# A hybrid attention layer on one core: per-unit maxima and delayed exponentials in the differential heads

## The chip, the core and the metric

The kernel runs as one program on one NeuronCore of one Trainium2 chip. The core has a matrix engine (TensorE, PE in the profile; its weight loads stand apart as PEld), a vector engine (VectorE, DVE), an activation engine (ScalarE, ACT), a Pool engine (GpSimd, POOL) and a queue for transfers (SyncE, SP). Each engine takes its own instructions strictly one after the other and waits on semaphores for the results of the others. The metric is the device time of one execution in microseconds, the median of several executions.

## The reference

One decoder layer for 2048 tokens of width 1024, all in float32. Two groups of attention heads read the same normalised input; only the first group matters here.

```
n  = rms_norm(x, norm_g)
dq, dk, dv, ... = split(n @ w_in)              # 4 differential heads, 2 maps each of width 64, values 128
q, k = rope(dq), rope(dk);  scale = 64 ** -0.5 # = 0.125
sc = einsum(q, k) * scale                      # two score maps m = 0, 1 per head
pr = softmax(where(k_idx <= q_idx, sc, -inf))  # causal
a  = pr[0] - lam * pr[1]                       # one learned lam
od = rms_norm(a @ v, subln_g) * 0.8, then * silu(gate)
... second group (latent attention, 8 heads), output projection, gated embedding, final norm
```

## The kernel before

The program runs in stages, one after the other: the input projection (0 to about 470 us), the up projections of the latent group (to about 650), latent attention (to about 1162), the differential heads (1162 to 1576), and the output stage (to 2040). Tiles come from pools with a fixed number of buffers; a compile-time scheduler puts each engine's instructions in order from the order in the source and from when it thinks their inputs are there, and sets all semaphores.

**Projection of queries and keys (L359 to L385).** For m = 0 (queries) and m = 1 (keys) the product of 512 tokens by 128 columns lands in PSUM tile `ps`; VectorE multiplies it by a cosine table (L375, one instruction) and by a sine table (L377, four instructions of 32 partitions), Pool adds both (L379), and the sum is split in two parts and stored.

**Differential heads (L810 to L1005).** Work comes in blocks `(h, b)`: head h, 128 query rows b, keys up to n = 128 (b + 1). `block` (L845) makes the unnormalised weights of one block. Its scores are computed in units of up to 1024 keys, so a block with b of 8 or more has two units per map (`nu` = 2), the others one. `unit(m, u)` (L854) multiplies queries with keys into the PSUM tile `pu` (1024 columns, three buffers, L816), and VectorE takes the row maximum (L874). Before, the units of one map come one after the other, and `expo(m)` (L876) follows when both are there: one small VectorE instruction turns the larger maximum into the bias (L880 for two units, L882 for one), and ScalarE takes the exponentials of both units with the scale 0.125 and sums them (L885). So the first unit's PSUM buffer is held until the second unit's maximum is known. `combine` (L888) runs after the first unit of the next block: sums (L891), reciprocals (L893), the factor `cc` (L895), and then map 0 plus `cc` times map 1: the last unit by VectorE (L902), a full first unit by Pool in two instructions (L899 multiplies map 1, L900 adds).

`weigh(h, g)` (L913) takes blocks 2g and 2g + 1: per 256 keys, `turn` transposes the weights on PE into the PSUM tile `tpa` (one buffer, L930), ScalarE copies it to `ah` (L932), and `mul` multiplies with the values (L942). At the end come a copy, a transpose, squares on ScalarE (L956), a power on Pool (L107) and two small pairs of VectorE instructions (L961, L962); the Pool power and those pairs are put in as `ends` at places 2 and 4 of the following task list (L991).

The main loop (L982) runs over 32 pairs (h, g); even heads go up in g, odd heads go down. In step i, `merge` weaves the tasks of `weigh` with those of two blocks that lie three ahead (`LEAD`), by their costs. During the last head the loads and splits of the output weights (L835 to L837) are woven in too. In the first head pair and again in the second, 16 blocks have two units, 32 in all; the other 32 blocks have one.

Of the kernel before, what the change touches and what calls it, by code (L numbers as in the profile page):

```python
# [8 lines left out]
F32 = mybir.dt.float32  # L9
# [4 lines left out]
ALU = mybir.AluOpType  # L14
# [11 lines left out]
LAM_INIT = 0.2  # L26
TWO_PI = 6.283185307179586
# [37 lines left out]
def tile_hymba(ctx, tc, a, out):  # L65
# [130 lines left out]
    with ExitStack() as c1:  # L196
# [162 lines left out]
        for m in range(2):  # L359
            wg, wn = wn, (load_w(512, 512) if m == 0 else load_w(2560, 272))  # L360
            for t in range(NT):
# [4 lines left out]
                for g in range(4):  # L366
# [8 lines left out]
                    V.tensor_mul(t1, pt, tcos)  # L375
                    for q in range(4):
                        V.tensor_mul(t2[32 * (q ^ 1):32 * (q ^ 1) + 32], pt[32 * q:32 * q + 32],  # L377
                                     tsin[32 * q:32 * q + 32])
# [431 lines left out]
    SC_D = 64.0 ** -0.5  # L810
    with ExitStack() as c3:
# [32 lines left out]

        def block(h, b):  # L845
# [8 lines left out]
            def unit(m, u):  # L854
                hd = heads[h]
                if m == 0 and u == 0:
                    st["s"] = sm.tile([P, 2, 2], F32, name="ssum", tag="ssum", bufs=4)
                if u == 0:
                    st[m] = pp.tile([P, S], F32, name="pb", tag=f"pb{m}", bufs=(6 if m == 0 else 2))
                    st["x", m] = sm.tile([P, 2], F32, name="mxd", tag="mxd", bufs=4)  # L860
                pu = ps_s.tile([P, 1024], F32, name="pu")
                st["u", m, u] = pu
# [11 lines left out]
                V.reduce_max(st["x", m][:, u:u + 1], pu[:, :w], axis=AX.X)  # L874

            def expo(m):  # L876
                mx, ssum = st["x", m], st["s"]
                nm = sm.tile([P, 1], F32, name="nm", tag="nm", bufs=4)
                if nu == 2:
                    V.tensor_scalar(nm, mx[:, 0:1], scalar1=mx[:, 1:2], scalar2=-SC_D, op0=ALU.max, op1=ALU.mult)  # L880
                else:
                    V.tensor_scalar_mul(nm, mx[:, 0:1], -SC_D)  # L882
                for u in range(nu):
                    w = min(1024, n - u * 1024)
                    A.activation(st[m][:, u * 1024:u * 1024 + w], st["u", m, u][:, :w], AF.Exp, scale=SC_D, bias=nm,  # L885
                                 accum_out=ssum[:, m, u:u + 1])

            def combine():  # L888
                ssum = st["s"]
                if nu == 2:  # L890
                    V.tensor_add(ssum[:, :, 0], ssum[:, :, 0], ssum[:, :, 1])  # L891
# [4 lines left out]
                for c in range(nu):  # L896
                    sl = slice(c * 1024, min(n, (c + 1) * 1024))
                    if c < nu - 1:
# [83 lines left out]
        for i, (h, g) in enumerate(order):  # L982
# [10 lines left out]
            if nxt is late:  # L993
                for _, f in late:
                    f()
# [164 lines left out]
```

## Time and profile before

The median of three runs is 2042.25 us (2040.35 to 2043.14). The profiled execution took 2042.74 us by itself; its span from the first to the last instruction is 2040.5 us, and some 2.2 us lie around it.

| engine | busy us | share of the span | instructions |
|---|---|---|---|
| PE (matmul) | 1930.3 | 95% | 9521 |
| PEld (weight load) | 1520.2 | 74% | 9521 |
| DVE | 1208.1 | 59% | 2685 |
| ACT | 917.7 | 45% | 2089 |
| POOL | 634.4 | 31% | 528 |

A busy PE is not PE at its peak: matmuls are pipelined, and the first one after a pause shows longer. What an engine waited for is listed by who ended the wait. A PE wait shows most fully on PEld, since the weight load is the first instruction that stops; PE itself still finishes what is in its pipeline.

### The profile page before, as it was taken

To read this page: it belongs to the slowest core of one execution; us is meant where nothing else is said; L and a number is where in the kernel's file an instruction comes from. 1 tells how busy PE (TensorE), PEld (TensorE's weight loads), DVE (VectorE), ACT (ScalarE), POOL (GpSimd) and SP (SyncE) were. 2 spreads that over 40 slices of the span, in tenths; PEclk is the share of its full clock that TensorE was granted. 3 is DMA by queue.
4 is the path that set the end of the run, shared out by engine and by line. 5 is a ranking of instruction groups with operands and counts; after the bars stand their busy time and mean duration, and the time that the engine had idled before them with its cause. 6 is when DMAs were issued, how large, how long until landed. Compare 5 with 4: busy or idle time off the path is not lost.

```text
span 2040.5 us, 28322 instructions
## 1 busy us (share of the span) xinstructions
PE 1930.3 (95%) x9521; PEld 1520.2 (74%) x9521; DVE 1208.1 (59%) x2685; ACT 917.7 (45%) x2089; POOL 634.4 (31%) x528
## 2 busy tenths in 40 slices
PE   7999999999999699999999989899988899999997
PEld 5788878898887477777777667676666677777786
DVE  5253677632446487888888687677876533333322
ACT  4422001122333467777777677677776311111111
POOL 4400345300000166666656335414441201111100
PEclk9999999999998899999999899999998999999999
DMA  5442333322267643514141311530021522222210
GB/s 165 140 147 87 130 127 135 119 86 77 65 211 255 219 127 105 144 55 130 31 118 42 101 35 43 154 112 27 24 83 56 194 90 68 88 88 88 75 47 21
DMA packets 171680, 209.73 MB, mean 103 GB/s; under 512 B 38876, under 2 KB 99180, under 8 KB 171536
## 3 DMA queue, kind: packets, MB, share of 16 engines
q1 hardware_dynamic: 171536, 207.93, 32.6%
q8 instruction: 75, 1.23, 0.3%
q14 instruction: 69, 0.57, 0.1%
HBM read 129.65 MB, written 78.14 MB: 102 GB/s over the span
## 4 chain that ended last, share of the span: by engine, by line
PE 75%; DVE 7%; ACT 7%; DMA 3%; POOL 2%; issue 2%; SPq 1%; ACTq 0%; POOLq 0%; DVEq 0%
PE p L1053 6%; PE p L1055 6%; PE p L1054 6%; PE ps L252 5%; PE ps L251 5%; PE ps L253 5%; PE pod L942 3%; PE pm L171 3%; PE po L704 3%; PE ps L372 3%; PE pst L675 3%; PE ps L370 3%; PE ps L371 3%; PE po L705 3%; PE pst L674 3%; PE pst L673 3%
## 5 line engine op out<-in xcount | busy, mean ns | idle before, releaser
L690 POOL TENSOR_TENSOR acc<-ph,acc 128x512 f32<-128x512 f32 (+3 forms) x208 | 216.6, 1041 | 165.2 <-DVE acc L685 76.2
L251 PE MATMUL ps<-wh,xh 128*128 128x512 f32 (+1 forms) x640 | 229.6, 359 | 9.6 <-DVE wh L240 7.9
L252 PE MATMUL ps<-wl,xh 128*128 128x512 f32 (+1 forms) x640 | 227.6, 356 | 0.5 <-DVE wl L241 0.4
L253 PE MATMUL ps<-wh,xl 128*128 128x512 f32 (+1 forms) x640 | 226.7, 356 | 0.4 <-DVE xl L228 0.3
L678 ACT ACTIVATE ph<-pst 128x512 fp32r<-128x512 f32 (+1 forms) x320 | 170.2, 532 | 114.1 <-PE pst L675 61.6
L695 DVE TENSOR_TENSOR pl<-pst,ph 128x512 fp32r<-128x512 f32 (+1 forms) x320 | 193.3, 607 | 45.7 <-ACT pst L679 42.9
L874 DVE TENSOR_REDUCE mxd<-pu 128x1 f32<-128x1024 f32 (+4 forms) x192 | 173.1, 908 | 61.9 <-PE pu L873 39.0
L885 ACT ACTIVATE pb<-pu,nm 128x1024 f32<-128x1024 f32 (+4 forms) x192 | 165.6, 866 | 39.3 <-DVE nm L880 25.7
L679 ACT ACTIVATE pst<-pst 128x512 f32<-128x512 f32 (+1 forms) x320 | 169.0, 528 | 0.0
L107 POOL TENSOR_TENSOR s<-s,half 128x2 f32<-128x2 f32 (+1 forms) x48 | 32.6, 679 | 425.0 <-DVE s L106 359.6
L870 PE MATMUL pu<-hd 128*128 128x512 f32 (+3 forms) x320 | 139.8, 437 | 20.6 <-ACT pb L885 17.6
L942 PE MATMUL pod<-ah,hd 128*128 128x256 f32 (+1 forms) x576 | 146.5, 379 | 0.5 <-ACT ah L934 0.5
L251 PEld LDWEIGHTS ps<-wh,xh 128*128 128x128 f32 x640 | 121.5, 190 | 30.2 <-ACT sq L223 6.6
L173 DVE TENSOR_REDUCE mx<-pm 128x1 f32<-128x512 f32 x192 | 130.0, 680 | 14.9 <-PE pm L171 14.8
L253 PEld LDWEIGHTS ps<-wh,xl 128*128 128x128 f32 x640 | 121.2, 190 | 20.1 <-DVE xl L228 2.7
L252 PEld LDWEIGHTS ps<-wl,xh 128*128 128x128 f32 x640 | 121.7, 190 | 18.9 <-DVE wl L241 1.8
L1102 DVE TENSOR_TENSOR sg<-p,sg 128x512 f32<-128x512 f32 (+1 forms) x34 | 20.8, 655 | 175.1 <-ACT sg L1101 175.1
L871 PE MATMUL pu<-hd 128*128 128x512 f32 (+3 forms) x320 | 122.6, 390 | 0.0
L704 PE MATMUL po<-ph,vall 128*128 128x512 f32 (+1 forms) x320 | 117.9, 374 | 4.8 <-ACT ph L678 4.5
L673 PE MATMUL pst<-QH,kall 97*128 97x512 f32 (+2 forms) x296 | 119.1, 402 | 0.0
L171 PE MATMUL pm<-kall,QH 96*128 96x512 f32 (+3 forms) x296 | 115.0, 403 | 3.6 <-DVE mx L173 2.5
L705 PE MATMUL po<-pl,vall 128*65 128x512 f32 (+1 forms) x320 | 115.4, 363 | 0.0
(265 smaller groups left out, 4735.1 us busy)
## 6 DMA issues: line engine op xcount, KB each, us to landing
hd<-dq_s SPq DMA_DIRECT2D x192, 128.0 KB
wr<-in_w_in SPq DMA_DIRECT2D x40, 256.0 KB
xr<-in_xT SPq DMA_DIRECT2D x32, 256.0 KB
dq_s<-th SPq DMA_DIRECT2D x32, 256.0 KB
dq_s<-tl SPq DMA_DIRECT2D x32, 256.0 KB
k_s<-stage SPq DMA_DIRECT2D x16, 512.0 KB
q_s<-stage SPq DMA_DIRECT2D x16, 512.0 KB
v_s<-stage SPq DMA_DIRECT2D x16, 512.0 KB
```

The lines of the kernel that those rows point to most:

```text
L171: T.matmul(pm[:, :w], lhsT=q, rhs=keys_of(pr, e, c)[0][0:96, :w], start=True, stop=True)
L251: T.matmul(pt[:, :w], lhsT=h, rhs=wh[k][:, :w], start=(k == 0), stop=False)
L252: T.matmul(pt[:, :w], lhsT=h, rhs=wl[k][:, :w], start=False, stop=False)
L253: T.matmul(pt[:, :w], lhsT=l, rhs=wh[k][:, :w], start=False, stop=(k == KT - 1))
L673: T.matmul(pt[:, o:], lhsT=kh[0:97], rhs=qh[0:97, o:], start=True, stop=False)
L678: A.activation(ph[:, o:], pt[:, o:], AF.Exp, scale=SC_M)
L690: eng.tensor_add(self.acc[:, o:], ph[:, o:].bitcast(F32), self.acc[:, o:])
L695: V.tensor_sub(pl[:, o:], pt[:, o:], ph[:, o:].bitcast(F32))
L704: T.matmul(self.po[:, o:], lhsT=vv[:, 0:128], rhs=ph[:, o:], start=(kc == 0), stop=(kc == self.n - 1))
L705: T.matmul(self.po2[:65, o:], lhsT=vv[:, 64:129], rhs=pl[:, o:], start=(kc == 0), stop=False)
L874: V.reduce_max(st["x", m][:, u:u + 1], pu[:, :w], axis=AX.X)
L942: T.matmul(st["po"][:, o:], lhsT=vv, rhs=st[u][:, i, o:], start=(kc == 0), stop=(kc == nk - 1))
```

## The change

The units of a block now come in the order of units first, maps second. VectorE writes the negated maximum of each unit straight from the reduction; for the second unit it takes the minimum of both negated maxima, a running maximum. Each unit has its own exponential, which is issued one unit later (`step` counts), with the maximum that its unit knew. `combine` comes two units after the block's last one. For two-unit blocks it takes the correction factor `f` = exp of the difference of both biases for both maps, multiplies the first unit's sums by it, and Pool now multiplies both maps of the first unit (by `f` and by `f` times `cc`) before it adds. The factor 0.125 moves from the exponentials into the projection: the products with the tables become `scalar_tensor_tensor` with 0.125 for queries and 1.0 for keys.

```
+SC_D = 0.125
...
-                    V.tensor_mul(t1, pt, tcos)
+                    sc = SC_D if m == 0 else 1.0
+                    V.scalar_tensor_tensor(t1, pt, sc, tcos, op0=ALU.mult, op1=ALU.mult)
                     for q in range(4):
-                        V.tensor_mul(t2[32 * (q ^ 1):32 * (q ^ 1) + 32], pt[32 * q:32 * q + 32],
-                                     tsin[32 * q:32 * q + 32])
+                        V.scalar_tensor_tensor(t2[32 * (q ^ 1):32 * (q ^ 1) + 32], pt[32 * q:32 * q + 32], sc,
+                                               tsin[32 * q:32 * q + 32], op0=ALU.mult, op1=ALU.mult)
...
+        def step(new=()):
+            for x in late:
+                x[0] -= 1
+            due = [x for x in late if x[0] <= 0]
+            late[:] = [x for x in late if x[0] > 0] + [list(x) for x in new]
+            for _, f in due:
+                f()
...
-                V.reduce_max(st["x", m][:, u:u + 1], pu[:, :w], axis=AX.X)
-
-            def expo(m):
-                mx, ssum = st["x", m], st["s"]
-                nm = sm.tile([P, 1], F32, name="nm", tag="nm", bufs=4)
+                nm = st["n"]
+                V.tensor_reduce(nm[:, m, u:u + 1], pu[:, :w], op=ALU.max, axis=AX.X, negate=True)
+                if u == 1:
+                    V.tensor_tensor(nm[:, m, 1:2], nm[:, m, 0:1], nm[:, m, 1:2], op=ALU.min)
+                def expo():
+                    A.activation(st[m][:, u * 1024:u * 1024 + w], pu[:, :w], AF.Exp, bias=nm[:, m, u:u + 1],
+                                 accum_out=st["s"][:, m, u:u + 1])
+                step([(1, expo)] + ([(2, combine)] if (m, u) == (1, nu - 1) else []))
+
+            def combine():
+                ssum, nm = st["s"], st["n"]
                 if nu == 2:
-                    V.tensor_scalar(nm, mx[:, 0:1], scalar1=mx[:, 1:2], scalar2=-SC_D, op0=ALU.max, op1=ALU.mult)
-                else:
-                    V.tensor_scalar_mul(nm, mx[:, 0:1], -SC_D)
-                for u in range(nu):
-                    w = min(1024, n - u * 1024)
-                    A.activation(st[m][:, u * 1024:u * 1024 + w], st["u", m, u][:, :w], AF.Exp, scale=SC_D, bias=nm,
-                                 accum_out=ssum[:, m, u:u + 1])
...
+                    f = sm.tile([P, 2], F32, name="f", tag="f", bufs=4)
+                    V.tensor_sub(f, nm[:, :, 1], nm[:, :, 0])
+                    A.activation(f, f, AF.Exp)
+                    V.tensor_mul(ssum[:, :, 0], ssum[:, :, 0], f)
                     V.tensor_add(ssum[:, :, 0], ssum[:, :, 0], ssum[:, :, 1])
                 rc = ...; V.reciprocal(rc, ssum[:, :, 0])
                 cc = ...; V.scalar_tensor_tensor(cc, ssum[:, 0, 0:1], rc[:, 1:2], neglam, op0=ALU.mult, op1=ALU.mult)
-                for c in range(nu):
-                    sl = slice(c * 1024, min(n, (c + 1) * 1024))
-                    if c < nu - 1:
-                        G.tensor_scalar(st[1][:, sl], st[1][:, sl], scalar1=cc, scalar2=0.0, op0=ALU.mult, op1=ALU.add)
-                        G.tensor_add(st[0][:, sl], st[0][:, sl], st[1][:, sl])
-                    else:
-                        V.scalar_tensor_tensor(st[0][:, sl], st[1][:, sl], cc, st[0][:, sl], op0=ALU.mult, op1=ALU.add)
+                if nu == 2:
+                    V.tensor_mul(f[:, 1:2], f[:, 1:2], cc)
+                    sl = slice(0, 1024)
+                    for m in range(2):
+                        G.tensor_scalar(st[m][:, sl], st[m][:, sl], scalar1=f[:, m:m + 1], scalar2=0.0, op0=ALU.mult,
+                                        op1=ALU.add)
+                    G.tensor_add(st[0][:, sl], st[0][:, sl], st[1][:, sl])
+                sl = slice((nu - 1) * 1024, n)
+                V.scalar_tensor_tensor(st[0][:, sl], st[1][:, sl], cc, st[0][:, sl], op0=ALU.mult, op1=ALU.add)
...
-            for m in range(2):
-                for u in range(nu):
-                    w = min(1024, n - u * 1024)
-                    tasks.append((w / 512 * 0.45, lambda m=m, u=u: unit(m, u)))
-                tasks.append((0.3, lambda m=m: expo(m)))
-            last, late[:] = late[:], [(0, combine)]
-            return tasks[:1] + last + tasks[1:]
+            for u, m in ((u, m) for u in range(nu) for m in range(2)):
+                w = min(1024, n - u * 1024)
+                tasks.append((w / 512 * 0.45 + 0.1, lambda m=m, u=u: unit(m, u)))
+            return tasks
```

## Rows read from the trace of the kernel before

**Rows 1.** Busy by stretch: us, PE, PEld, DVE, ACT, POOL (instructions), clock, DMA.
```profile
205.00:392.00 187.00, 185.59 (x808) 149.13 (x807) 129.94 (x196) 19.94 (x32) 81.50 (x62) 1.00 0.37 128
1162.00:1576.00 414.00, 367.43 (x1950) 281.80 (x1950) 311.34 (x731) 300.95 (x779) 157.02 (x97) 0.97 0.23 67
1194.00:1329.00 135.00, 123.10 (x648) 94.69 (x647) 93.66 (x189) 94.70 (x221) 70.30 (x39) 0.99 0.27 77
1394.00:1539.00 145.00, 124.58 (x638) 94.40 (x638) 113.45 (x218) 104.07 (x253) 73.42 (x41) 0.98 0.13 42
1324.00:1327.50 3.50, 3.50 (x14) 2.74 (x13) 1.43 (x5) 0.58 (x1) 2.72 (x2) 0.51 0.42 128
```

**Rows 2.** Waits, 1162 to 1576: waiter <- who ended it: us in total, times, longest.
```profile
PEld pu L870 <- ACT pb L885: 34.4, 59, 1.7
...
PEld tpa L930 <- ACT ah L932: 31.5, 56, 3.7
ACT pb L885 <- DVE nm L880: 25.7, 23, 3.4
...
PEld tpa L930 <- POOL pb L900: 2.6, 8, 0.6
```

**Rows 3.** Groups by line and shape, 1162 to 1576: busy us, mean ns | idle before.
```profile
L874 DVE TENSOR_REDUCE mxd<-pu 128x1 f32<-128x1024 f32 x80 | 97.5, 1219 | 34.9 <-PE pu L871 21.8 <-PE pu L873 12.4
...
L900 POOL TENSOR_TENSOR pb<-pb 128x1024 f32<-128x1024 f32 x32 | 77.1, 2411 | 2.7
...
L899 POOL TENSOR_SCALAR pb<-pb,cc 128x1024 f32<-128x1024 f32 x32 | 54.2, 1693 | 98.0 <-DVE cc L895 45.3 <-DVE nm L880 33.7 <-ACT wo L836 6.0
...
L956 ACT ACTIVATE junkd<-zo,rc 128x128 f32<-128x128 f32 x62 | 24.8, 401 | 1.2
...
L880 DVE TENSOR_SCALAR nm<-mxd 128x1 f32<-128x1 f32 x64 | 13.5, 211 | 1.0
...
L902 DVE SCALAR_TENSOR_TENSOR pb<-pb,cc 128x1024 f32<-128x1024 f32 x8 | 10.7, 1337 | 0.2
...
L882 DVE TENSOR_SCALAR nm<-mxd 128x1 f32<-128x1 f32 x64 | 9.1, 148 | 0.5
```

**Rows 4.** Single lines: duration ns min/median/max, first and last start, shapes.
```profile
L961 DVE TENSOR_TENSOR s<-s,rc x64: 140/154/1223, 1175.8 to 1579.4; 128x1 f32<-128x1 f32 x64
...
L962 DVE SCALAR_TENSOR_TENSOR ztd<-zo,s,sg x64: 330/347/2528, 1176.1 to 1581.0; 128x128 f32<-128x128 f32 x64
...
L899 POOL TENSOR_SCALAR pb<-pb,cc x32: 1117/1672/2271, 1194.5 to 1535.0; 128x1024 f32<-128x1024 f32 x32
```

**Rows 5.** Timeline near 1527: start, us, engine, line, operation.
```profile
1526.81 2.53 DVE L962 SCALAR_TENSOR_TENSOR ztd<-zo,s,sg 128x128 f32<-128x128 f32 x1
1526.83 2.36 POOL L900 TENSOR_TENSOR pb<-pb 128x1024 f32<-128x1024 f32 x1
```

**Rows 6.** Timeline, 1321 to 1324.
```profile
1321.73 1.11 ACT L885 ACTIVATE pb<-pu,nm 128x1024 f32<-128x1024 f32 x1 [3.40 <-DVE nm L880]
...
1323.46 0.66 PE L930 MATMUL tpa<-ident,pb 128*128 128x128 f32 x4 [3.33 <-ACT ah L932]
```

**Rows 7.** Timeline, 1254 to 1257.
```profile
1254.14 2.37 POOL L900 TENSOR_TENSOR pb<-pb 128x1024 f32<-128x1024 f32 x1
...
1255.60 0.21 DVE L880 TENSOR_SCALAR nm<-mxd 128x1 f32<-128x1 f32 x1
...
1256.56 0.31 PEld L930 LDWEIGHTS tpa<-ident,pb 128*128 128x128 f32 x3 [0.22 <-POOL pb L900]
```

**Rows 8.** Lines of the projections: duration ns min/median/max; the wait ahead of L375.
```profile
L375 DVE TENSOR_TENSOR t<-ps,tcos x32: 682/692/692, 212.1 to 390.0; 128x512 f32<-128x512 f32 x32
...
  PE ps L372: 44.5, 22
...
L377 DVE TENSOR_TENSOR t<-ps,tsin x128: 679/686/696, 212.8 to 392.8; 32x512 f32<-32x512 f32 x128
...
L228 DVE SCALAR_TENSOR_TENSOR xl<-xr,norm_g,xh x32: 739/752/1747, 5.4 to 90.5; 128x512 fp32r<-128x512 f32 x32
```

More of the change, by code (lines that the diff above doesn't have):

```diff
@@ L807, in mix @@
             G.tensor_mul(zg[:, g * 512:(g + 1) * 512], zg[:, g * 512:(g + 1) * 512], gt[:, g * 512:(g + 1) * 512])
-    SC_D = 64.0 ** -0.5
     with ExitStack() as c3:
@@ L857, in unit @@
                     st["s"] = sm.tile([P, 2, 2], F32, name="ssum", tag="ssum", bufs=4)
+                    st["n"] = sm.tile([P, 2, 2], F32, name="nm", tag="nm", bufs=4)
                 if u == 0:
                     st[m] = pp.tile([P, S], F32, name="pb", tag=f"pb{m}", bufs=(6 if m == 0 else 2))
-                    st["x", m] = sm.tile([P, 2], F32, name="mxd", tag="mxd", bufs=4)
                 pu = ps_s.tile([P, 1024], F32, name="pu")
-                st["u", m, u] = pu
                 w = min(1024, n - u * 1024)
@@ L873, in unit @@
                         T.matmul(o[:, cw - P:cw], lhsT=ident_b, rhs=mask_b, start=False, stop=True)
-                V.reduce_max(st["x", m][:, u:u + 1], pu[:, :w], axis=AX.X)
-            def expo(m):
-                mx, ssum = st["x", m], st["s"]
-                nm = sm.tile([P, 1], F32, name="nm", tag="nm", bufs=4)
-                if nu == 2:
-                    V.tensor_scalar(nm, mx[:, 0:1], scalar1=mx[:, 1:2], scalar2=-SC_D, op0=ALU.max, op1=ALU.mult)
-                else:
-                    V.tensor_scalar_mul(nm, mx[:, 0:1], -SC_D)
-                for u in range(nu):
-                    w = min(1024, n - u * 1024)
-                    A.activation(st[m][:, u * 1024:u * 1024 + w], st["u", m, u][:, :w], AF.Exp, scale=SC_D, bias=nm,
-                                 accum_out=ssum[:, m, u:u + 1])
-            def combine():
-                ssum = st["s"]
-                if nu == 2:
+                nm = st["n"]
[8 more added lines that the diff above has]
+                ssum, nm = st["s"], st["n"]
+                if nu == 2:
+                    f = sm.tile([P, 2], F32, name="f", tag="f", bufs=4)
+                    V.tensor_sub(f, nm[:, :, 1], nm[:, :, 0])
+                    A.activation(f, f, AF.Exp)
+                    V.tensor_mul(ssum[:, :, 0], ssum[:, :, 0], f)
                     V.tensor_add(ssum[:, :, 0], ssum[:, :, 0], ssum[:, :, 1])
@@ L989, in tile_hymba @@
             nxt = [x for y in blocks[LEAD + 2 * i:LEAD + 2 * i + 2] for x in block(*y)]
-            nxt = nxt or late
+            while not nxt and late:
+                step()
             for n, f in zip((2, 4), ends):
                 nxt.insert(n, (0, f))
-            if nxt is late:
-                for _, f in late:
-                    f()
-                nxt = []
             if i == len(order) - 2:
```

## The prediction, made before the changed kernel was run

> **What bounds the kernel now.** I read first the busy time by stretch. Between 1162 and 1576 us, the differential heads, PE is busy 367 of 414 us and no other engine more than 311 [rows 1]: PE sets the pace, and there are 47 us in which it is idle. All of Pool's multiplications, one for each of the 32 two-unit blocks, start between 1194.5 and 1535.0 [rows 4], so two stretches hold them: 1194 to 1329 and 1394 to 1539, together 280 us. There PE is busy 247.7 us (88%), VectorE 207.1 (74%), ScalarE 198.8 and Pool 143.7 [rows 1]. I call them the heavy stretches. Then I read who waits for whom: PE's weight loads stand 34.4 us in 59 waits for an exponential to give back a score buffer, and 31.5 us in 56 waits for ScalarE's copy of transposed weights; ScalarE itself stands 25.7 us in 23 waits before an exponential, for the bias of a two-unit map [rows 2]. The reader is to see one chain here: with three score buffers, two are held until the second unit's maximum is known, then ScalarE works off two exponentials in a row, and copies queued behind them come late. Once the chain breaks badly: ScalarE waits 3.40 us for a bias, PE then 3.33 us for a copy [rows 6], and the granted clock of the stretch just behind is 0.51, the 1.2 GHz level [rows 1].
>
> **The change part by part.** The sum is made against the profiled execution's own 2042.7 us.
>
> *Projection, 160 multiplications become three-operand ones.* A multiplication from PSUM takes 0.69 us, the nearest three-operand instruction of that width 0.75 [rows 8]: 160 by 0.06 is 10 us of VectorE, 32 by 5 by 0.06. VectorE is busy 130 of 187 us there, PE 185.6, and VectorE waits for PE 44.5 us before the first multiplication of a group [rows 1, 8]. It is hidden, even at the row's longest, 1.75 us for one; price zero. Were the cover gone, 10 us would be added. Dropping the scale in the exponential is worth nothing either way, since the instruction stays.
>
> *Exponentials per unit, one unit behind.* A score buffer is now free after its own maximum and its own exponential, not after the second unit's. This goes for both maps of the 32 blocks, and the order of units first leaves a whole unit between the two maxima of a map. The 34.4 us of waits for buffers can vanish at most; nothing excludes a loss of their size if ScalarE's queue, with an exponential behind each unit's copies, holds buffers as long as before. I take three quarters, **-26 us**: what the next unit's matmuls leave as time for a 1.22 us reduction [rows 3] is enough in most places, not in all. What is late next is the reduction, then the copy. ScalarE's waits for a bias stop heads of its queue, so some of the 31.5 us of waits for copies goes too; bounds are zero and the whole. I take the one break of [rows 6] with what its low clock costs, 3.33 plus half of 3.5 us: **-5 us**.
>
> *Small instructions.* 64 bias instructions of 0.211 us go from the heavy stretches and 64 of 0.148 from the others [rows 3]. Added are 64 minima and, in 32 blocks, a difference and two products: 160 instructions near the 0.154 us median of a two-input one on a column [rows 4], 24.6 us. VectorE gains 11 us in the heavy stretches and loses 9.5 in the others. ScalarE gets 32 exponentials of two columns; the nearest row is an activation of 128 columns at 0.40 us [rows 3], so at most 13 us against 81 us idle.
>
> *Pool multiplies both maps.* 32 more multiplications, 1.69 us on average, 1.12 at least [rows 3, 4]: 36 to 54 us on an engine that is idle 136 of 280 us. Two things depend on it. First, the chain to `turn`: PE's first transposes of a pair need Pool's sum, and there is no slack, since Pool's addition ends at 1256.51 and the transposes start at 1256.56 after a wait [rows 7]; 8 such weight-load waits are 2.6 us together [rows 2]. Now `combine` is issued a unit later and Pool has an instruction more. Against that, only one exponential instead of two lies between the last maximum and `combine`, and Pool's first product needs `f` alone, not `cc`. Of the 16 pairs I charge a quarter of the added 1.12 us at each: **+4 us**; bounds zero and 16 by 1.69 plus a reduction, 47 us.
>
> *VectorE behind Pool.* At 1526.81 a small product of two SBUF operands takes 2.53 us instead of its usual 0.35, and ends 0.15 us behind Pool's addition, which began 0.02 us after it [rows 4, 5]; a one-column one has taken 1.22 us instead of 0.15 [rows 4]. The old bias instruction, with one tensor input, took its 0.21 us in the middle of a Pool addition [rows 7]. So the change replaces an instruction that Pool doesn't hold up by one that it does. Pool will run 1.12 + 1.12 + 2.36 = 4.6 us for a block, 147 of 280 us, 53%. An instruction that comes at any time finds on average half the length of the one it meets, weighted by length: (1.12² + 1.12² + 2.36²) / (2 by 4.6) = 0.88 us, so 0.46 us for each of 64 minima, 30 us. The sum in `combine` follows `f` as Pool's first product does, and can stand up to 1.1 us behind it: half of that in 32 blocks, 18 us. With the 11 us above VectorE needs 207 + 11 + 48 = 266 of 280 us. Its 73 idle us cover 59, on paper; but it is strictly in order, and what is behind a held minimum is the next unit's reduction. I put a quarter on the path, **+15 us**; bounds zero and all 59.
>
> The Trainium skill, SBUF — State Buffer, "Who interferes with whom", says that VectorE and GpSimd share a port pair under an exclusive lock, so that a two-input vector operation and a Pool operation exclude each other for a whole instruction. By that rule the trace agrees (2.53 us beside 2.36), and every one of the 64 minima is exposed; the sum's 48 us would then lean to the path, which is the third case below.
>
> Sum: -26 - 5 + 4 + 15 = -12, hence 2030.7 us for a profiled execution and, since that one lay 0.5 us above the median, **2030 us**. The other 32 blocks, without Pool work, add nothing to it: their 9.5 us of VectorE lie beside PE.
>
> **The rivals.** Two per mille, 4 us, is about what a measurement of this kernel can tell from no change.
> - *Deeper.* The minima are held where nobody waits, since each exponential is due a unit later anyway. Then only the +4 stands against -31, and the other exposed copies' waits give some 6 more: 2009 us. For it: VectorE idles mostly for PE's scores, 34.9 us ahead of the widest reduction [rows 3]. Against it: PE is busy 88% already, and the copies' single buffer stays.
> - *No change.* PE's waits change their name: what no longer stands for a score buffer stands for a copy, since transposes have one buffer and ScalarE is busy 71%. The gain of 31 is eaten by as much: 2042 us.
> - *Slower: VectorE becomes the bound.* Its place is the running minimum in the heavy stretches, its price 48 us of held instructions plus 11. If VectorE then reaches no higher share than PE now, 88%, 266 us of work take 301 instead of 280: +21, less some 10 us of waits that go in other blocks and at breaks: 2053 us. It decides once held time passes some two thirds of what I computed, since 207 + 11 + 30 at 88% is 280. For it: in-order queues, and Pool's run falls behind `combine`, where the next block's second units come. The rule named above would give this time, and is its strongest witness. Against it: an exponential has a unit of slack.
> - *Pool's chain is the bound.* `combine` a unit later and a product more, 16 turns late by some 3 us: +48 less 30, 2060 us. Against it: the scheduler can put two of the next units first.
>
> **How the numbers follow.** Forecast 41% (its own range 2019 to 2037), deeper 15%, no change 17%, VectorE bound 21%, Pool's chain 6%. Faster by over 4 us: the first two without a small edge, 55%; within 4 us, 17%; slower: the last two and that edge, 28%. The range for 8 in 10 reaches from 2006, below the deeper case, to 2054, just above the VectorE case, and leaves out Pool's chain and the tails.
>
> **What would show it.** Right, if PE's waits for `pu` fall below 10 us, ScalarE's waits for a bias nearly vanish, Pool shows 64 multiplications, the minima show a mean well above 0.15 us with longest near 2.4, and the stage is some 12 us shorter while all others keep their times. The prediction is wrong if VectorE's busy time in the stage passes 370 us of 414 and PE's waits for `pu` stay, or if the transposes' waits for Pool's addition grow above 20 us; deeper, if the minima stay near 0.15 us.

## The result and the profile after

The changed kernel takes 2067.46 us (median of four, 2066.78 to 2072.6), the kernel before 2042.7 beside it: a ratio of 1.0127, 95% interval 1.0106 to 1.0147, that is 26 us slower (22 to 30). The forecast was 12 us faster.

All of it lies in the differential heads. The stretch of the projection has the same busy times as in [rows 1]; the last small product of the heads starts at 1609.3 us instead of 1579.4 [rows 4], and the span is 30.3 us longer. The profiled execution is the longest of the four, 2072.6 us, so its rows show some 5 us more than the median. First the busy time by stretch of the changed kernel (columns as in [rows 1]), the projection, the stage and its two heavy stretches:

```profile
205.00:392.00 187.00, 185.57 (x806) 148.94 (x806) 129.71 (x196) 19.97 (x32) 81.64 (x62) 1.00 0.37 128
...
1162.00:1606.00 444.00, 376.54 (x1951) 291.49 (x1952) 363.74 (x765) 305.27 (x811) 190.75 (x129) 0.94 0.21 63
1194.00:1344.00 150.00, 128.00 (x660) 99.41 (x660) 123.11 (x235) 97.34 (x241) 86.73 (x55) 0.95 0.24 69
1402.00:1570.00 168.00, 136.22 (x668) 106.35 (x667) 142.78 (x274) 109.63 (x280) 91.71 (x58) 0.91 0.12 36
```

The heavy stretches take 318 us where [rows 1] have 280. VectorE is busy in them for 123.11 + 142.78 = 265.9 us, and the prediction had said 266: what VectorE would have to do was right in sum. PE is idle 67.5 us of the stage instead of 47, and its busy time is 9.1 us longer at a granted clock of 0.94 instead of 0.97. This 0.94 is a mean of two levels. At one place, for example, the clock falls during a wait of 1.93 us for Pool's addition (1476.72 to 1478.65 us) and stands at 0.50, the 1.2 GHz level, from 1478.4 to 1484.0; a score matmul of 512 columns takes 0.63 us there and 0.40 a little later, at 2.4 GHz. So a part of what such a wait costs comes behind it, as longer PE work. Next the groups of small instructions and of Pool's (columns as in [rows 3]):

```profile
L910 POOL TENSOR_SCALAR pb<-pb,f 128x1024 f32<-128x1024 f32 x64 | 89.6, 1400 | 124.2 <-ACT f L899 74.0 <-DVE f L907 45.0 <-issue 5.1
...
L912 POOL TENSOR_TENSOR pb<-pb 128x1024 f32<-128x1024 f32 x32 | 76.1, 2379 | 2.7
...
L886 DVE TENSOR_TENSOR nm<-nm 128x1 f32<-128x1 f32 x64 | 36.6, 577 | 0.8
...
L901 DVE TENSOR_TENSOR ssum<-ssum 128x2 f32<-128x2 f32 x32 | 18.9, 592 | 0.6
...
L898 DVE TENSOR_TENSOR f<-nm 128x2 f32<-128x2 f32 x32 | 13.5, 422 | 0.8
...
L900 DVE TENSOR_TENSOR ssum<-ssum,f 128x2 f32<-128x2 f32 x32 | 7.6, 237 | 14.5 <-ACT f L899 14.2
```

An instruction of this kind that nothing holds takes 0.154 us [rows 4]. What lies above it in these four groups is counted as held time: 64 by 0.423 us for the minima (L886), 27 us; 32 by 0.438 for the sum's addition (L901), 14 us; 32 by 0.268 for the difference (L898), 8.6; 32 by 0.083 for the product (L900), 2.7: 52 us. The prediction computed 48 (30 and 18), without the difference. Two pieces of the timeline (columns as in [rows 5], in brackets what the engine waited for) show what holds:

```profile
1250.63 0.24 ACT L899 ACTIVATE f<-f 128x2 f32<-128x2 f32 x1
...
1250.90 0.16 DVE L900 TENSOR_TENSOR ssum<-ssum,f 128x2 f32<-128x2 f32 x1
...
1250.97 1.12 POOL L910 TENSOR_SCALAR pb<-pb,f 128x1024 f32<-128x1024 f32 x1 [0.99 <-ACT f L899]
1251.10 1.00 DVE L901 TENSOR_TENSOR ssum<-ssum 128x2 f32<-128x2 f32 x1
...
1252.66 1.14 DVE L914 SCALAR_TENSOR_TENSOR pb<-pb,cc 128x896 f32<-128x896 f32 x1
1252.84 1.96 POOL L910 TENSOR_SCALAR pb<-pb,f 128x1024 f32<-128x1024 f32 x1 [0.75 <-DVE f L907]
...
1254.88 2.38 POOL L912 TENSOR_TENSOR pb<-pb 128x1024 f32<-128x1024 f32 x1
...
1255.99 1.35 DVE L886 TENSOR_TENSOR nm<-nm 128x1 f32<-128x1 f32 x2
...
1257.31 1.11 ACT L889 ACTIVATE pb<-pu,nm 128x1024 f32<-128x1024 f32 x1 [2.21 <-DVE nm L886]
...
1258.57 0.50 PE L879 MATMUL pu<-hd 128*128 128x512 f32 x1 [1.06 <-ACT pb L889]
```

The addition of two columns begins 0.13 us behind Pool's first product and ends 0.01 us behind it, after 1.00 us. Two minima end 0.08 us behind Pool's addition; ScalarE has stood 2.21 us before the exponential for them, and PE then 1.06 us for the score buffer. At 1252.84 it is the other way: VectorE's product began first, and Pool's takes 1.96 us instead of 1.12 and ends 1.00 us behind it. Last, who waits for whom (columns as in [rows 2]):

```profile
ACT pb L889 <- DVE nm L886: 46.1, 28, 3.7
...
PEld tpa L939 <- ACT ah L941: 35.9, 53, 4.8
PEld pu L879 <- ACT pb L889: 31.3, 34, 3.1
ACT pb L889 <- DVE nm L884: 25.8, 26, 4.2
...
DVE ssum L900 <- ACT f L899: 14.2, 12, 2.8
PEld tpa L939 <- POOL pb L912: 12.6, 10, 2.1
```

Against [rows 2], PE's waits for score buffers have hardly fallen (31.3 from 34.4), its waits for copies have risen (35.9 from 31.5) and those for Pool's addition too (12.6 from 2.6). ScalarE stands 46.1 us for minima, where it stood 25.7 for the old bias, and 25.8 us more for reductions.

### The profile page after: what moved, and what is told of

It is laid out like the page before. It is cut to its first block, busy times and chain, and to the rows that moved or that the text cites. A ratio compares the mean times of both kernels' runs of the same rounds, so it can differ in the third digit from the quotient of the medians.

```text
span 2070.8 us, 28398 instructions
## 1 busy us (share of the span) xinstructions
PE 1938.3 (94%) x9521; PEld 1529.9 (74%) x9521; DVE 1259.4 (61%) x2717; ACT 922.5 (45%) x2121; POOL 669.0 (32%) x560
## 4 chain that ended last, share of the span: by engine, by line
PE 70%; DVE 11%; ACT 5%; POOL 3%; DMA 3%; issue 3%; SPq 1%; ACTq 0%; DVEq 0%; POOLq 0%
PE p L1059 6%; PE p L1061 6%; PE p L1060 6%; PE ps L253 5%; PE ps L252 5%; PE ps L254 5%; PE pm L172 3%; DVE nm L884 3%; PE po L706 3%; PE pst L677 3%; PE pst L675 3%; PE pst L676 3%; PE po L707 3%; PE ps L373 3%; PE ps L371 3%
## 5 line engine op out<-in xcount | busy, mean ns | idle before, releaser
L889 ACT ACTIVATE pb<-pu,nm 128x1024 f32<-128x1024 f32 (+4 forms) x192 | 166.8, 870 | 85.1 <-DVE nm L886 46.1
L884 DVE TENSOR_REDUCE nm<-pu 128x1 f32<-128x1024 f32 (+4 forms) x192 | 172.4, 907 | 38.3 <-PE pu L880 22.1
L879 PE MATMUL pu<-hd 128*128 128x512 f32 (+3 forms) x320 | 145.5, 455 | 23.6 <-ACT pb L889 21.3
L910 POOL TENSOR_SCALAR pb<-pb,f 128x1024 f32<-128x1024 f32 x64 | 89.6, 1400 | 124.2 <-ACT f L899 74.0
L1108 DVE TENSOR_TENSOR sg<-p,sg 128x512 f32<-128x512 f32 (+1 forms) x34 | 20.8, 655 | 175.5 <-ACT sg L1107 175.5
L880 PE MATMUL pu<-hd 128*128 128x512 f32 (+3 forms) x320 | 127.0, 402 | 0.0
L939 PE MATMUL tpa<-ident,pb 128*128 128x128 f32 x544 | 95.6, 295 | 32.9 <-ACT ah L941 20.4
```

The source lines that it names most:

```text
L884: V.tensor_reduce(nm[:, m, u:u + 1], pu[:, :w], op=ALU.max, axis=AX.X, negate=True)
L889: A.activation(st[m][:, u * 1024:u * 1024 + w], pu[:, :w], AF.Exp, bias=nm[:, m, u:u + 1], accum_out=st["s"][:, m, u:u + 1])
```

## The experiments

Each kernel was run together with the kernel before on one chip; a difference in us is (ratio minus 1) by 2042.7, with the ends of the 95% interval. Two kernels are compared by these differences. Theory H: small VectorE instructions with two tensor inputs are held by Pool's, and that takes the gain and more. Its rivals are Pool's longer chain to the transposes, the later combination, and the new order of work.

| kernel | us against before | interval |
|---|---|---|
| changed kernel | +25.9 | +21.7 to +30.0 |
| a_ts_min | +14.9 | +11.8 to +18.0 |
| b_ts_all | -10.0 | -13.3 to -6.7 |
| c_pool_short | +1.6 | -0.4 to +3.7 |
| d_early | +16.3 | +13.3 to +19.4 |
| k_old_tt | +12.1 | +8.0 to +16.1 |
| f_ts_early | -4.3 | -6.5 to -2.0 |
| g_ts_nodelay | -10.4 | -13.5 to -7.1 |
| i_ts_short | -13.5 | -17.2 to -10.0 |
| n_tt_min | +2.7 | +0.8 to +4.7 |
| o_ts_more | -6.9 | -9.6 to -4.3 |
| h_ts_morder | -11.6 | -16.1 to -7.4 |
| e_scale | +0.6 | -1.4 to +2.5 |
| p_diff_ts | +1.0 | -1.0 to +2.9 |
| q_tt_sum | +1.2 | -1.4 to +3.9 |
| r_tt_diff | +7.8 | +5.3 to +10.2 |

### a_ts_min: the minima alone with one tensor input

```
-V.tensor_tensor(nm[:, m, 1:2], nm[:, m, 0:1], nm[:, m, 1:2], op=ALU.min)
+V.tensor_scalar(nm[:, m, 1:2], nm[:, m, 1:2], scalar1=nm[:, m, 0:1], scalar2=1.0,
+                op0=ALU.min, op1=ALU.mult)
```

> The changed kernel, with the running minimum as an operation with one tensor input and a column operand instead of two tensor inputs. Held theory (small VectorE instructions with two SBUF inputs stand behind Pool's operations): the 64 minima fall from 0.577 us on average to about 0.21, 23 us of VectorE go, ScalarE's wait for a bias falls from 72 us to below 45, and the time from 2067 to about 2055. Pool-chain theory (Pool's third operation and the later combination make the first transposes late): no change, 2063 to 2070.

It came 11 us below the changed kernel, as theory H had it. ScalarE's waits for a bias fell less than it said, from 72 us to 56 (29.5 for minima, 26.7 for reductions), not below 45. The minima take 0.209 us each and are held no more, but the next instruction with two inputs in VectorE's queue is: the difference (L898) went from 0.422 to 0.699 us on average, 8.9 us of held time that moved rather than vanished. The sum's addition was held less, 0.471 us instead of 0.592.

### b_ts_all: no small instruction of the units with two tensor inputs

```
+(the minimum as in a_ts_min)
-V.tensor_sub(f, nm[:, :, 1], nm[:, :, 0])
-A.activation(f, f, AF.Exp)
-V.tensor_mul(ssum[:, :, 0], ssum[:, :, 0], f)
-V.tensor_add(ssum[:, :, 0], ssum[:, :, 0], ssum[:, :, 1])
+for m in range(2):
+    A.activation(f[:, m:m+1], nm[:, m, 0:1], AF.Exp, scale=-1.0, bias=nm[:, m, 1:2])
+    V.tensor_scalar(ssum[:, m, 0:1], ssum[:, m, 0:1], scalar1=f[:, m:m+1],
+                    scalar2=ssum[:, m, 1:2], op0=ALU.mult, op1=ALU.add)
-V.tensor_mul(f[:, 1:2], f[:, 1:2], cc)
+V.tensor_scalar(f[:, 1:2], f[:, 1:2], scalar1=cc, scalar2=1.0, op0=ALU.mult, op1=ALU.mult)
```

> The changed kernel with no small two-input instruction left on VectorE in units and combinations: minima, sums and the product f times cc take one tensor and column operands, and the difference of the biases is taken inside ScalarE's exponential, one for each map. Pool's work is as in the changed kernel. Held theory: VectorE's busy time in the stage falls by about 50 us and the time to 2035 to 2045. Pool-chain theory: the transposes' wait for Pool's addition stays at 10 us or more and the time above 2058.

This is 36 us below the changed kernel and 10 below the kernel before, with Pool's third instruction, the order and the delay as in the changed kernel. That is more than H had given it (2035 to 2045), although VectorE's busy time in the stage fell by 40 us (363.74 to 324.17), not 50. Its rows, first the single minima (columns as in [rows 4]), then stage, groups and waits, in the columns above:

```profile
L886 DVE TENSOR_SCALAR nm<-nm x64: 198/208/216, 1186.8 to 1517.9; 128x1 f32<-128x1 f32 x64
```
```profile
1162.00:1569.00 407.00, 363.48 (x1949) 283.27 (x1949) 324.17 (x730) 311.69 (x845) 189.85 (x129) 0.97 0.23 69
```
```profile
L910 POOL TENSOR_SCALAR pb<-pb,f 128x1024 f32<-128x1024 f32 x64 | 88.5, 1384 | 84.4 <-DVE f L907 54.5 <-ACT f L899 24.6 <-issue 5.3
...
L899 ACT ACTIVATE f<-nm 128x1 f32<-128x1 f32 x64 | 18.0, 300 | 0.0
...
L900 DVE TENSOR_SCALAR ssum<-ssum,f 128x1 f32<-128x1 f32 x64 | 16.3, 266 | 9.9 <-ACT f L899 9.8
```
```profile
ACT pb L889 <- DVE nm L884: 28.9, 33, 4.8
PEld tpa L939 <- ACT ah L941: 26.1, 49, 2.9
...
PEld pu L879 <- ACT pb L889: 20.8, 39, 1.6
...
ACT pb L889 <- DVE nm L886: 14.1, 15, 2.8
...
PEld tpa L939 <- POOL pb L912: 9.5, 8, 2.1
```

Pool works as long as in the changed kernel (88.5 us of products), yet the longest of 64 minima is 0.216 us. The Trainium skill, SBUF — State Buffer, "Who interferes with whom", says that a vector instruction with at most one SBUF input, outside the 2-port performance modes, does not contend with GpSimd. This run agrees (0.216 us at most, with Pool busy 190 of 407 us), and the column operand does not count as such an input here. PE's waits for score buffers fall to 20.8 us, not to the 8 of the prediction. Without a hold the new form is the slower one, 0.208 us against the 0.159 of the old form's median. The run changes the form of four things at once: the minimum, the sum, the difference and the product of `f` and `cc`. The last was not held in the changed kernel (0.156 us on average); the last four experiments take the other three apart.

### c_pool_short: without Pool's product of map 0

```
-for m in range(2):
+for m in (1,):
     G.tensor_scalar(st[m][:, sl], ...)
```

> The changed kernel without Pool's multiplication of map 0 by f: this factor is left out of the output. Pool is left with its two operations of before. Held theory: Pool runs 3.5 us for a block instead of 4.6, so held time falls by about a quarter and the time to about 2060; the sum behind Pool's first product is no longer held (0.59 us to 0.16), which may make it 2055. Pool-chain theory: the transposes' wait for Pool falls from 12.6 us to below 4 and the time to 2045 or less.

24 us below the changed kernel, for 39 us less of Pool's products (50.8 instead of 89.6). The time, 2042 us, is what the Pool-chain theory gave (2045 or less) and not H's 2055 to 2060. But that theory's sign did not come: the transposes wait as long for Pool's addition as in the changed kernel, 11.7 us against 12.6. What fell is the group of the sum's addition (columns as in [rows 3]):

```profile
L901 DVE TENSOR_TENSOR ssum<-ssum 128x2 f32<-128x2 f32 x32 | 5.1, 159 | 0.6
```

From 0.592 us it came down to 0.159: it no longer stands behind Pool's first product, which now waits for `f` times `cc`. The minima are held less too, 0.490 us on average instead of 0.577, and the sum's product not at all (0.156). With the difference as it was, held time is 22 us less in sum, near the 24. That speaks for what the product held and against Pool's chain; what the product itself costs is asked again in i_ts_short.

### d_early: the combination one unit earlier

```
-step([(1, expo)] + ([(2, combine)] if (m, u) == (1, nu - 1) else []))
+step([(1, expo)] + ([(1, combine)] if (m, u) == (1, nu - 1) else []))
```

> The changed kernel with the combination issued one unit after a block's last one instead of two, right behind the last exponential. Held theory: no fewer held instructions, 2062 to 2072. Pool-chain theory: Pool's sum is ready some 2 us earlier in each of 16 turns, the transposes' wait falls below 5 us, and the time to about 2050.

10 us below the changed kernel, 2057 us, which neither theory had: H said 2062 to 2072, the Pool chain about 2050 with the transposes' wait below 5 us, and that wait is 9.5 us. The minima and the differences are held less (0.531 and 0.353 us on average), the sum's product more (0.291) and its addition as before (0.594): 3 us less in all. So the holds in these rows don't explain the 10 us. f_ts_early asks whether the chain does.

### k_old_tt: the held minimum in the order of before

```
 (the kernel before, with the scale in the queries)
-V.tensor_scalar_mul(nm, mx[:, 0:1], -1.0)         # blocks with one unit: now the reduction's output is the bias
-V.reduce_max(mx[:, u:u+1], pu[:, :w], axis=AX.X)
+V.tensor_reduce(mx[:, u:u+1], pu[:, :w], op=ALU.max, axis=AX.X, negate=True)
-V.tensor_scalar(nm, mx[:, 0:1], scalar1=mx[:, 1:2], scalar2=-1.0, op0=ALU.max, op1=ALU.mult)
+V.tensor_tensor(mx[:, 1:2], mx[:, 0:1], mx[:, 1:2], op=ALU.min)      # this is the bias
```

> The kernel before with its own order of work, Pool's two instructions and its exponentials as they were; the scale sits in the queries, the maxima come out negated, and the bias of a two-unit map is the minimum of two columns as an instruction of two tensor inputs (64 of them) in place of one with one tensor input and a column operand. Held theory: Pool runs 1.12 + 2.36 us for a block, 40% of the 280 us of the heavy stretches, and a minimum that comes at any time finds half of what it meets, 0.98 us: 0.39 us each, 25 us for 64. ScalarE stands before both exponentials of the map for each of them, so most of it is on the path: 10 to 25 us slower than before, 2053 to 2067, with the mean of these minima above 0.4 us and the longest near 2.4. Rival, the order of work and Pool's third instruction cost the time and held minima are hidden: within 4 us of before.

12 us slower than before (8 to 16), inside the bounds of H and outside the rival's. The group of the minima and the waits of this kernel (columns as in [rows 2, 3]; here the exponential is L885, the first score matmul L871):

```profile
L882 DVE TENSOR_TENSOR mxd<-mxd 128x1 f32<-128x1 f32 x64 | 22.5, 352 | 0.9
```
```profile
PEld pu L871 <- ACT pb L885: 51.1, 64, 3.5
...
ACT pb L885 <- DVE mxd L882: 41.0, 35, 4.7
```

64 by (0.352 - 0.154) is 13 us of held time, less than the 25 estimated (a mean above 0.4 us was expected), and about all of it arrives at the end: PE's waits for score buffers rose from 34.4 [rows 2] to 51.1 us. Holds elsewhere moved too and nearly cancel: the small products L961 take 18.1 us instead of 9.2, the splits of the output weights 17.1 instead of 22.9. Besides the form of the minimum, only the 64 bias instructions of the one-unit blocks went (9.1 us [rows 3]), and the scale, which e_scale prices at nothing. So this is H without the change's other parts, with Pool's work and the order of work as before.

### e_scale: the scale in the queries alone

```
 (the kernel before)
-V.tensor_mul(t1, pt, tcos)
+V.scalar_tensor_tensor(t1, pt, sc, tcos, op0=ALU.mult, op1=ALU.mult)   # and the four with tsin
...                                                                     # bias by -1, exponential without scale
```

> The kernel before with nothing but the scale moved into the queries: the 160 multiplications of the projection become three-operand ones, the bias is scaled by -1, the exponential by nothing. If they are hidden, as the prediction has it, no change: within 4 us of before, 2037 to 2045, and the stretch from 205 to 392 us as long as before. If they lie on the path of the projection: up to 10 us slower, 2045 to 2052. It is also the control for the run that put the held minimum into the order of before.

No change, as expected, and the control for k_old_tt. The projection's stretch (columns as in [rows 1]) is the one of before:

```profile
205.00:392.00 187.00, 185.58 (x817) 149.55 (x816) 130.35 (x197) 19.25 (x31) 82.32 (x63) 1.00 0.37 128
```

### f_ts_early, g_ts_nodelay, h_ts_morder, i_ts_short, o_ts_more: one change each on b_ts_all

```
f:  [(2, combine)]  ->  [(1, combine)]
g:  step([(1, expo)] + [(2, combine)])  ->  expo(); step([(1, combine)])      # at a block's last unit
h:  for u in range(nu) for m in range(2)  ->  for m in range(2) for u in range(nu)
i:  for m in range(2): G.tensor_scalar(...)  ->  for m in (1,): G.tensor_scalar(...)
o:  cc and s4 * rc as tensor_scalar with column operands
```

> The changed kernel with no small instruction of two tensor inputs left on VectorE for the units (minimum, sum and factor have one tensor input and column operands, the difference is taken inside ScalarE's exponential), and the combination issued one unit after a block's last, not two. If the transposes' waits for Pool's addition are still on the path (9.5 us of them with the combination late), the earlier combination gives what it gave the changed kernel, 10 us: 2021. If those 10 us were only fewer collisions of held instructions with Pool, nothing is left to gain: 2028 to 2033, as without the earlier combination.

f is 6 us slower than b (4 us either way), where d had been 10 faster than the changed kernel; neither case had that. The transposes' wait for Pool's addition is 10.3 us against 9.5. So an earlier combination brings nothing by the chain here, and what gave d its 10 us stays open.

> The same without held instructions, but each exponential is issued right behind its own unit's maximum instead of a unit later, the combination one unit after the block's last. It asks what the delay is worth. If the delay hides the maximum and the minimum (ScalarE then does not stand before an exponential): its removal gives ScalarE's bias waits back, 96 two-unit instances of some 1.3 us less what its other work covers, so 10 to 40 us slower than with the delay, 2040 to 2070, with ScalarE's waits for a bias above 80 us. Rival: the scores wait for buffers anyway, and the earlier exponential gives them back sooner: 2025 to 2033, with PE's waits for buffers below 20 us.

g is where b is (-10.4 against -10.0): the delay of the exponentials by a unit is worth nothing that could be measured, and the first expectation was wrong. The rival's time came, its sign only nearly (20.6 us instead of below 20). Its waits (columns as in [rows 2]):

```profile
ACT pb L889 <- DVE nm L884: 30.7, 34, 4.2
...
PEld pu L879 <- ACT pb L889: 20.6, 35, 3.2
...
ACT pb L889 <- DVE nm L886: 16.6, 13, 3.8
```

ScalarE stands 47 us for a bias without the delay, and 43 with it (28.9 and 14.1 in b).

> The version without held instructions with the order of units by map, as in the kernel before (both units of map 0, then both of map 1), all else as it is. It asks whether the order matters: two units of one map follow one another, so the second's running minimum comes one unit behind the first reduction, and exponentials still go one unit behind. If the unit between the two maxima of a map is what gives the gain: 5 to 10 us slower, 2037 to 2042. Rival, only the separate exponentials count: within 4 us, 2028 to 2035.

h is not slower than b either (-11.6): the order of units is not what gives the 10 us.

> The changed kernel without held instructions (one tensor input for minimum, sum and factor, the difference inside ScalarE's exponential), and without Pool's multiplication of map 0 by its factor, which is left out of the output. It prices that third Pool instruction where it holds nothing up. Held theory: it was dear (25 us) by what it held, so here it is worth 0 to 5 us: 2027 to 2032. Rival, Pool's chain to the transposes: each of the 16 pairs gets its sum 1.1 us earlier or more, 10 to 18 us, 2013 to 2021, and the transposes' waits for Pool's addition fall below 4 us.

i prices Pool's third instruction where it holds nothing up: 3.5 us, with intervals that also allow none. Of the 24 us of c_pool_short some 21 were then not the product itself. The transposes' wait for Pool's addition is 9.5 us, as in b: the rival's sign did not come.

> The version without held instructions, where also the factor cc of every block and the small products of a head pair's end become instructions with one tensor input and column operands. What was left of held time there is 64 by 0.035 us for cc and 64 by 0.04 for the products, 5 us. Held theory, at the share of seven tenths seen so far: 3 to 4 us less, 2027 to 2029. Rival, those products stand at the end of a chain that nobody waits for: 2030 to 2033, no change.

o, aimed at 5 us of held time, gave nothing that can be told from b.

### n_tt_min, q_tt_sum, r_tt_diff, p_diff_ts: the parts put back one by one

On b_ts_all:

```
n:  the 64 minima as V.tensor_tensor again
q:  the sum as V.tensor_mul and V.tensor_add again
r:  f as V.tensor_sub, then one A.activation(f, f, AF.Exp)
p:  f as two V.tensor_scalar(nm1, scalar1=nm0, op0=ALU.subtract, ...), then one A.activation(f, f, AF.Exp)
```

> The changed kernel with only the 64 running minima as instructions of two tensor inputs; sums, factor and difference stay free of them, as in the version that was faster than before. It asks which held instructions are dear. If the price goes by held time: the minima were held 27 us in the changed kernel, and 51 us of held time cost some 36, so 15 to 22 us more than with none, 2047 to 2054, with the mean of the minima at 0.5 to 0.6 us. If the instructions of the combination make the harm (with the minima alone freed, 24 us of the 36 stayed): 8 to 13 us, 2040 to 2045.

n costs 12.7 us against b, the second case: the minima are held 29 us, about what was expected, and less than half of it arrives. Their group (columns here and in the next two as in [rows 3]) shows 64 by 0.455 us of held time:

```profile
L886 DVE TENSOR_TENSOR nm<-nm 128x1 f32<-128x1 f32 x64 | 38.8, 609 | 0.9
```

> The version without held instructions, except that the two steps of the sum (times f, plus the second unit's) are instructions of two tensor inputs again; the difference stays inside ScalarE's exponential. It prices the hold of the sum behind Pool's first product alone. With the minima freed these two were held 15 us; at the share of three quarters that all held instructions of the combination showed there (24 of 32 us): 11 us, 2039 to 2046. If the difference alone made that price: 2029 to 2035.

q costs 11.2 us against b, as computed, but not for the reason computed: its two steps are held 5.6 and 2.6 us, 8 in all and not 15. The 11.2 is known to 4 us, so the 8 may be all of it; if not, no row shows what the rest is.

```profile
L900 DVE TENSOR_TENSOR ssum<-ssum,f 128x2 f32<-128x2 f32 x32 | 10.5, 328 | 4.8 <-ACT f L899 4.8
...
L901 DVE TENSOR_TENSOR ssum<-ssum 128x2 f32<-128x2 f32 x32 | 7.5, 235 | 0.7
```

> The version without held instructions, except that the difference is one instruction of two tensor inputs again, before one exponential for both maps. With the minima freed it was held 18 us: at three quarters 13 us, 2040 to 2048. If the sum behind Pool's product made the price: 2029 to 2036, and if only the hand-off counts, as much as the run with a difference that is not held.

r costs 17.8 us against b, with a difference that is held 32 by 0.561, 18 us:

```profile
L898 DVE TENSOR_TENSOR f<-nm 128x2 f32<-128x2 f32 x32 | 22.9, 715 | 0.8
```

> The version without held instructions, except that the difference of the two maxima is taken on VectorE again, as two instructions with one tensor input and a column operand, and handed to one exponential of ScalarE for both maps. So it has the hand-off from VectorE to ScalarE and back of the changed kernel, and nothing that Pool holds. If holding is what the combination cost: within 4 us of the version without it, 2028 to 2036. If the hand-off is: ScalarE stands before the small exponential with copies and exponentials queued behind, and it takes back a good part of the 24 us, 2039 to 2050.

p is the surprise: it costs 11.0 us against b (7 to 15), all of the gain, and nothing that it puts back is held. So of r's 17.8 only 6.8 are the hold of the difference. The single differences of p (columns as in [rows 4]) and its waits (as in [rows 2]; Pool's products are L913 here, its addition L915, the transposes L942):

```profile
L899 DVE TENSOR_SCALAR f<-nm x64: 194/207/215, 1187.9 to 1531.7; 128x1 f32<-128x1 f32 x64
```
```profile
POOL pb L913 <- ACT f L901: 43.2, 20, 7.0
...
ACT ah L944 <- PE tpa L942: 30.3, 27, 2.7
...
PEld tpa L942 <- POOL pb L915: 18.8, 12, 2.5
PEld pu L879 <- ACT pb L889: 18.1, 35, 1.3
```

No difference takes more than 0.215 us. But the transposes wait 18.8 us for Pool's addition instead of 9.5, and ScalarE's copies 30.3 us for the transposes instead of 17.1, while the waits for score buffers are no longer than in b. Pool idles as long ahead of its products as in b (84.5 and 84.4 us), but more of it for the exponential `f`, 43.2 us instead of 24.6. This is the hand-off: the difference takes its turn in VectorE's queue, then the exponential its turn in ScalarE's, before Pool's first product may start. In b the exponential takes both maxima itself and needs no further instruction of VectorE. That the 9 us of transposes' waits are the 11 us is a reading of the rows; no run took those waits away alone.

The traces show one thing more that p brings back with the hand-off. Its one exponential serves both maps, so Pool's product of map 0 must wait for the maximum of map 1 too; b has an exponential for each map. In 11 of 32 blocks of b the first product starts before the block's last minimum has ended, in p in none. One of these blocks in b (columns as in [rows 5]; L910 is Pool's product of map 0, L886 the minimum of map 1):

```profile
1237.09 1.12 POOL L910 TENSOR_SCALAR pb<-pb,f 128x1024 f32<-128x1024 f32 x1
...
1237.45 0.20 DVE L886 TENSOR_SCALAR nm<-nm 128x1 f32<-128x1 f32 x1
```

On average the first product starts 3.05 us behind the last minimum in p and 1.17 in b, and Pool's addition ends 9.79 and 9.11 us behind it. How much of the 11 us is the joint exponential, how much the way through two queues, and how much the 13 us of work that the 64 differences add to VectorE, no run separates. In what follows "the hand-off" means all of it.

The four parts add up to 12.7 + 11.2 + 11.0 + 6.8 = 41.7 us, and together they are 35.9. Each is known to some 4 us, and held time moves on to the next instruction (a_ts_min), so they need not add up. The shares differ widely: 12.7 of 29 us held for the minima, 6.8 of 18 for the difference, about all for the sum and in k_old_tt.

## Why the prediction was wrong

It said -12 and the runs say +25.9, 38 us apart. Three terms carry this.

*"I put a quarter on the path, +15 us" (VectorE behind Pool).* This step failed. The held time was right (48 computed, 52 measured), and so was VectorE's work (266 and 265.9 us). The share was not: the parts that only hold cost 12.7 + 11.2 + 6.8, 31 us put back one by one, or 25 when the hand-off's 11 is taken from the 36 of all: half to three fifths of 52. I argued with VectorE's idle time as cover, "on paper". But in the old order 12 of 13 us arrived (k_old_tt), where VectorE had about as much idle time as before (busy 318 us of 414, not 311). I read this so: what counts is who stands behind the held instruction (ScalarE before the exponential, PE before the buffer), not VectorE's sum. The runs show the shares, and that one share for all is wrong; why they differ was not tested. The third case of the prediction (VectorE as the bound) had 21%, and its time, 2053, was still 14 too low. The Trainium skill, SBUF — State Buffer, "Who interferes with whom", names the rule that the prediction set beside that case, an exclusive lock that is held for a whole instruction; the rows agree (1.00 us for an addition of two columns that ended 0.01 us behind Pool's product). The difference's hold (8.6 us in the changed kernel) was not in the list at all; I had counted its instruction and not its exposure.

*"ScalarE gets 32 exponentials of two columns ... at most 13 us against 81 us idle."* Failed. The exponentials themselves are short (32 by some 0.21 us, 6.7 us), but the hand-off round them costs 11 us (p_diff_ts). I priced an instruction by its duration and forgot the two queues that a block's factor must pass between the last maximum and Pool, and that one exponential for both maps waits for the later map.

*"Exponentials per unit ... I take three quarters, -26 us."* The waits fall, by half of what was taken: with nothing held, PE's waits for buffers fall from 34.4 to 20.8, 13.6 us. Neither the delay (g) nor the order of units (h) changes the time in these runs, so the reason that the prediction gave, a unit's time for the reduction, does not show in them. ScalarE still stands 28.9 us before exponentials for reductions. What keeps the other 20 us of buffer waits was not settled.

The smaller terms: the waits for copies fell 5.4 us in b, where -5 was taken. For Pool's chain +4 was taken: the third product costs 3.5 us (i_ts_short), the waits for Pool's addition rose 6.9 in b and did not fall without that product, so the size was near and the reason given for it holds only in part. -13.6, -5.4 and +6.9 make -12.1, and b has -10.0; waits need not turn into time one for one, so this is a check of size and no proof. The projection at nothing was right (e_scale).

So the forecast without held instructions, -27, would have been -10, and the holding and the hand-off put 36 on top. Of the signs for being right, Pool's 64 multiplications and the long minima came (0.577 us on average, 2.353 at most); PE's waits for `pu` (31.3 us, not below 10) and ScalarE's for a bias (72 us, not near none) did not. Of the signs that the prediction gave against itself, one came: PE's waits for `pu` stayed. VectorE's busy time, 363.7 us, stayed below the mark of 370, and the transposes' waits for Pool's addition, 12.6, below the 20: marks on totals were too coarse, the mean of the held instructions and ScalarE's waits for them told more.

The version without held instructions and without the hand-off (b_ts_all) beats both kernels, 2031.5 us, 0.5% below before (0.3 to 0.7); g and h can't be told from it.

## What to carry to other kernels

Before a small VectorE instruction is put beside a busy Pool, count its SBUF tensor inputs: written with one tensor and a column operand it was not held at all; with two it waited, where it met a Pool instruction, for that to end. About half of all that waiting came out at the end of the kernel, and between two fifths and all of it where one kind of instruction was tried by itself. Don't cover held time with an engine's idle sum; ask which engine stands behind the held instruction, since its whole queue stands with it. And price a step that crosses two engines by the queues it passes and by what it waits for: 0.2 us instructions, handed from VectorE to ScalarE and on to Pool, with one exponential for both maps, cost 11 us over 32 blocks. Taking the difference inside an exponential for each map gave them back.

## What the runs showed of the hardware

In these runs the holding goes by the number of tensor inputs in SBUF, not by size: one column out of two columns took up to 2.353 us, Pool's whole addition, while the same minimum with a column operand never passed 0.216 us and the reductions out of PSUM kept 1.22 us in all kernels. It is mutual: Pool's product took 1.96 us behind a VectorE product that had begun 0.18 us earlier. And held time moves: with the minima freed, the next instruction of two inputs in VectorE's queue rose from 0.422 to 0.699 us.

```profile
L886 DVE TENSOR_TENSOR nm<-nm x64: 142/159/2353, 1189.5 to 1560.2; 128x1 f32<-128x1 f32 x64
```
